# A two-layer decoder step: the first part's last norm woven between the second part's output products, a bias table from 5 products instead of 12, and other ranks for the streams

## The chip, the cores and the metric

The kernel runs on one core of one Trainium2 chip. The metric is device time in microseconds (us), from the first to the last instruction of one execution and the little that lies around it; a lower number is better. Of the kernel before there are three timed runs and one execution recorded by the profiler.

The core has five engines that run side by side, each through its own queue in order: TensorE (PE in the rows, PEld is its weight load), VectorE (DVE), ScalarE (ACT), GpSimd (POOL) and SyncE (SP), which here issues the DMAs. An instruction waits at the head of its queue until semaphores say that its inputs are written and its buffer is free, and everything behind it on that engine waits with it.

## The reference, cut to what matters

Layer 0 mixes tokens by attention, layer 1 by RWKV-7; both attend to 256 memory tokens, gate, and project to the model width of 1024. The work is 512 tokens of a prompt and 8 samples of 4 new tokens, 544 columns in all. What the change touches:

```python
logits = jnp.where(valid[None, None], logits + bias[None, :, None, :], NEG_INF)   # layer 0, attention bias
...
S = S * w_t[:, :, None, :] + sa[..., None] * b_t[:, :, None, :] + v_t[..., None] * k_t[:, :, None, :]  # layer 1
...
h = jnp.concatenate([y, o_mem], axis=-1) * jax.nn.silu(gate)
return h @ w_out, cols[:, -1], S.astype(xn.dtype)
...
xp = xp + rms_norm(hp, norm_post[i])          # after each layer, over the 1024 features
```

The three places are the bias of the samples' new keys in layer 0, the order of layer 1's streams, and layer 1's last norm and residual.

## The kernel before

Activations lie with features on the 128 partitions and the 544 tokens along the free side, so a projection of 1024 to 128 features is eight k-tiles, each of three products: weights and activations are split into a high and a low part (`hi`, `lo`), and `mm1` multiplies high by high, low by high and high by low (L311 to L313). `split_piece` (L297 to L304) loads a weight piece, casts the high part on ACT and subtracts on POOL.

Layer 0 begins with the memory tokens, cross attention and the projections `a{n}`. The bias tables are made on PE at 117 to 124 us, between the products of a projection: `SB` for the cached keys (L715, L716) and `SN` for the samples' new keys. For `SN` the kernel runs over two groups of 4 samples (`bg`) and three window groups (`j`); each pair takes a product of the table `lg` with a one-hot block (L722) and a product of the mask `negsel` with `bad` (L723), each of 32 columns. All of these are plain fp32, so each shows twice in the trace.

Layer 1 is a set of generators, called streams, each with a rank. The planner `Flow` picks the stream with the lowest rank that is ready, advances a clock by the time that the stream states, and so writes one program; `LAT` holds the delays after which a stream counts as ready again, `RANK` the ranks, `GORDER` the order of the eight gate columns, `GEARLY` how many of them may come before the last column. The engines then run the written order. For each of three groups of four heads (`g` = 0, 1, 2) the streams are:

- `scores`, `products`: the chunk matrices `SA`, and their triangular inverse by 30 steps on DVE, two instructions per step (`TX`, L1445, and `T`, L1447);
- `recur`: the state `St` over 8 chunks, with products `z` and `y` (L1631);
- `sample`: the samples' states (`zs`, `us`, `sts`, L1594), then their norm; `norm`, `normed`: the group norm of `y`, written to `bv`.

The dense work that fills PE between them is the columns `b{n}`, the gates `b1{j}_` and, at the end, the output projection. `outer` prepares its inputs: `gated(j)` reads the gate `ug{j}` back from DRAM, multiplies (L1757, DVE), casts to `h1` (L1758, ACT) and subtracts the low part (L1759, on DVE for `j` in `LOD`, else on POOL). The `o1` products use heads of groups 0 and 1; `last(i)` adds those of group 2 for part `i` of the tokens (0: 256 columns, 1: 288): eight products `o2{mt}{i}` added to `z` on DVE (L1791), squares on ACT (L1793), their sum on POOL (L1796) and PE (L326), the reciprocal root (`pow`, L339, on POOL; `rvx`, L346, on ACT; `rs_p`, L353, on PE), and for each of eight tiles a multiplication (L1805, DVE), the residual's addition (L1806, on DVE for `kt` in `RADD`, else on POOL) and an output DMA (L1807, issued by SP).

In `last` the finish of part 0 stands as one block, ahead of the products of part 1 in the program:

```python
rp = rstd_of(acc, n, lambda name: zs[:, 512:1024] if i else ps_t(name), f"p1{i}", eps=4e-6)
yield 0.2, 2.0
for kt in range(8):
    nc.vector.scalar_tensor_tensor(z[kt], z[kt], vec("post1", kt), rp, ALU.mult, ALU.mult)
    (nc.vector if kt in RADD else nc.gpsimd).tensor_tensor(z[kt], z[kt], xr[kt], ALU.add)
    nc.sync.dma_start(O["y"][:, kt, ts], z[kt])
```

Of the kernel before, what the change touches and what calls it, by code (L numbers as in the profile page):

```python
# [16 lines left out]
ALU = mybir.AluOpType  # L17
# [4 lines left out]
TMPB = 6  # L22
WLV = (2, 3, 4, 7)
SQB, XNB = 9, 2
GORDER = (6, 2, 0, 1, 7, 3, 4, 5)
COLB = 5
HB = 3
RAWB = 2
RAWO = 3
XRB = 14  # L30
OFF = {0: 0, 8: 0, 9: -200, 10: -200}
SQ1 = 6
RADD = (0, 3, 6)
ET = mybir.EngineType
D, A, G = ET.DVE, ET.Activation, ET.Pool
MENG = set(), set(), set()
# [1 line left out]
LOP = (0, 3, 4)  # L38
WOB = 10
DU = 2  # L40
GEARLY = 7
LAT = [4.0, 5.82, 0.4, 0.6, 5.42, 5.2, 1.5, 0.94, 2.61, 0.6, 1.2]
RANK = [4, 2, 7, 3, 2, 4, 6, 9]
RHO, DEBT = 0.35, 0.5
LOD = [7]
KB = 4
CCB = 8
PB_ = 4
# [6 lines left out]
PART = (slice(0, 256), slice(256, NT))  # L55
# [3 lines left out]
GORD = (1, 2, 0)  # L59
# [170 lines left out]
def _device(tc, I, O):  # L230
# [20 lines left out]
    def ps_t(name):  # L251
        return psum[0].tile([128, 512], F32, tag="t", bufs=2, name=name)
# [30 lines left out]
    def vec(name, j):  # L283
        s = PV[name]
        return pv[:, s.start + j:s.start + j + 1]
# [36 lines left out]
    def add_squares(acc, sq, n, first, last):  # L322

        for i in (0, 256, 128) if n > 256 else (0, 128):
            w = min(128, n - i)
            nc.tensor.matmul(acc[0:w, i // 128:i // 128 + 1], sq[:, i:i + w], ones[:, 0:1],  # L326
                             start=first and i == 0, stop=last and i == 128)
# [30 lines left out]
    def rstd_of(acc, n, bank, name, out=None, eps=1e-6):  # L358
        return rstd_end(rstd_mid(rstd_begin(acc, n, name, eps), n, name), n, bank(f"rs_{name}"), out)
# [319 lines left out]
    with ExitStack() as pro:  # L679
        pm = pool(pro, "bias", 1)  # L680

        ohp = pm.tile([33, 9 * 256], F32, name="ohp")
        rel = pm.tile([33, 12], F32, name="rel")
        nc.sync.dma_start(ohp, I["ohp"])
        nc.vector.memset(rel[32:33, :], NEG)
        nc.sync.dma_start(rel[0:32, :], I["rel"])
        bv = pm.tile([4, 9 * 256], F32, name="bv")
        for a, b, g in ((0, 512, 0), (512, 1024, 0), (1024, 1536, 0), (1536, 1792, 0), (1792, 2048, 1), (2048, 2304, 2)):
            ps = ps_t(f"bv{a}")
            nc.tensor.matmul(ps[0:4, :b - a], rel[:, g * 4:g * 4 + 4], ohp[:, a:b], start=True, stop=True)  # L690
            nc.vector.tensor_copy(bv[:, a:b], ps[0:4, :b - a])
        bd = pdr.tile([4, 9 * 256], F32, name="bd")
        nc.sync.dma_start(bd, bv)
        for h in range(4):
            t = bd[h:h + 1, :]
            nc.sync.dma_start(PB[:, h].rearrange("p (m k) -> p m k", m=9),
                              bass.AP(tensor=t.tensor, offset=t.offset, ap=[[1, 128], [256, 9], [1, 128]]))

        ohs = pm.tile([128, 1248], F32, name="ohs")
        bad = pm.tile([32, 1248], F32, name="bad")  # L700
        negsel = pm.tile([32, 256], F32, name="negsel")
        rel4 = pm.tile([128, 12], F32, name="rel4")
        dt4 = pm.tile([128, 4], F32, name="dt4")
        lg = pm.tile([128, 3, 4, 8, 4], F32, name="lg")
        for t, n in ((ohs, "ohs"), (bad, "bad"), (negsel, "negsel"), (rel4, "rel4"), (dt4, "dt4")):
            nc.sync.dma_start(t, I[n])
        nc.vector.memset(lg, 0.0)
        for g in range(3):
            nc.vector.tensor_tensor(
                lg[:, g, :, 0:4, :],  # L710
                rel4[:, None, g * 4:g * 4 + 4, None].to_broadcast([128, 4, 4, 4]),
                dt4[:, None, None, :].to_broadcast([128, 4, 4, 4]), ALU.mult)
        for g, a, b in ((1, 0, 512), (2, 512, 1024), (0, 1024, 1152)):
            ps = ps_t(f"sb{g}")
            nc.tensor.matmul(ps[:, :b - a], lg[:, g].rearrange("p a b c -> p (a b c)"), ohs[:, a:b], start=True, stop=False)  # L715
            nc.tensor.matmul(ps[:, :b - a], negsel[:, 0:128], bad[:, a:b], start=False, stop=True)  # L716
            nc.scalar.copy(SB[:, a:b], ps[:, :b - a])
        for bg in range(2):
            ps = ps_t(f"sn{bg}")
            for j, g in enumerate(GORD):  # L720
                a = 1152 + 32 * j
                nc.tensor.matmul(ps[:, 32 * j:32 * j + 32], lg[:, g].rearrange("p a b c -> p (a b c)"), ohs[:, a:a + 32], start=True, stop=False)  # L722
                nc.tensor.matmul(ps[:, 32 * j:32 * j + 32], negsel[:, bg * 128:bg * 128 + 128], bad[:, a:a + 32], start=False, stop=True)  # L723
            nc.scalar.copy(SN[:, bg], ps[:, :96])

    def attention(f, pat):

# [381 lines left out]
    def tmp(name):  # L1109
        return pp.tile([128, NT], F32, tag="tmp", bufs=TMPB, name=name)  # L1110
# [656 lines left out]
            rows.append(tmp(f"{name}7")[:, 0:n])  # L1767
        return t, rows

    def last(i):  # L1770

        n, ts = (256, 288)[i], PART[i]
        z, h1 = out.z[i], out.h1
        t, xr = by_row(i, "SA", 2048, "xr1")
        m = 7 + (not i)
        nc.sync.dma_start(t[:, 0:m * n].rearrange("p (k t) -> p k t", t=n), x1d[:, 0:m, ts])
        if i:
            nc.sync.dma_start(xr[7], x1d[:, 7, ts])
        for j in (4, 5):
            gated(j, (i,))  # L1780
        yield 0.0, 2.0
        zs = ps_zs("ssz11") if i else None
        acc = zs[:, 0:512] if i else ps_t("ssz10")
        sqs = []
        for mt in range(8):
            ps = ps_mm(f"o2{mt}{i}")
            for k in range(2):
                a = (mt % 2 * 2 + k) * 128
                mm1(ps, out.w2h[:, mt // 2, a:a + 128], out.w2l[:, mt // 2, a:a + 128],
                    h1[:, 0, 4 + k, ts], h1[:, 1, 4 + k, ts], n, k == 0, k == 1)  # L1790
            nc.vector.tensor_tensor(z[mt], z[mt], ps[:, :n], ALU.add)  # L1791
            sq = tmp(f"sqo1{mt}{i}")[:, 0:n]
            nc.scalar.activation(sq, z[mt], AF.Square)  # L1793
            sqs.append(sq)
            if 0 < mt < SQ1:
                nc.gpsimd.tensor_tensor(sqs[0], sqs[0], sq, ALU.add)  # L1796
            if mt > SQ1:
                add_squares(acc, sqs[mt - 1], n, mt == SQ1 + 1, False)
            yield 0.75, 0.2
        add_squares(acc, sqs[0], n, False, False)  # L1800
        add_squares(acc, sqs[7], n, False, True)
        rp = rstd_of(acc, n, lambda name: zs[:, 512:1024] if i else ps_t(name), f"p1{i}", eps=4e-6)
        yield 0.2, 2.0
        for kt in range(8):
            nc.vector.scalar_tensor_tensor(z[kt], z[kt], vec("post1", kt), rp, ALU.mult, ALU.mult)  # L1805
            (nc.vector if kt in RADD else nc.gpsimd).tensor_tensor(z[kt], z[kt], xr[kt], ALU.add)  # L1806
            nc.sync.dma_start(O["y"][:, kt, ts], z[kt])  # L1807
            yield 0.0, 0.7

    def outer():  # L1810
# [129 lines left out]
```

## Time and profile before

| what | us |
| --- | --- |
| median of three runs | 816.17 (813.39 to 816.59) |
| the profiled execution's own time | 817.52 |
| its span, first to last instruction | 815.7 |
| PE busy | 757.4 (93%) |
| DVE busy | 465.9 (57%) |
| POOL busy | 351.4 (43%) |
| ACT busy | 338.9 (42%) |

The busy times are sums over the whole span. The profile cuts the span into 40 slices of about 20 us; a digit is the busy share of a slice in tenths, and the row PEclk gives the clock that the throttle granted to TensorE, also in tenths of full speed. Full speed is 2.4 GHz, half is 1.2 GHz. 1.82 us of the execution lie outside the span.

### The profile page before, as it was taken

The numbers are of one execution on the slowest core, as the hardware profiler recorded it, in microseconds if no ns is written. First come the engines' busy times: TensorE is split into PE (matmuls) and PEld (weight loads), VectorE is DVE, ScalarE is ACT, GpSimd is POOL, SyncE is SP. The second block draws the span as 40 slices with busy tenths as digits, with TensorE's granted clock in tenths as the row PEclk, the third lists the DMA queues.
The fourth block names the chain that finished last, engine by engine and source line by source line (L and its number), as shares of the span: only waits on it lengthen the run. The fifth ranks groups of instructions, "written<-read, shape, count | busy, mean of one in ns | idle before, by whom it ended". The sixth has DMA issues, their size and how long they took to land.

```text
span 815.7 us, 20095 instructions
## 1 busy us (share of the span) xinstructions
PE 757.4 (93%) x8278; PEld 643.7 (79%) x8278; DVE 465.9 (57%) x1095; ACT 338.9 (42%) x780; POOL 351.4 (43%) x388
## 2 busy tenths in 40 slices
PE   6999999999998997989999999999989999699883
PEld 5877778889875785678988889888879988498773
DVE  7643311237457556664365478945599547862485
ACT  7445311224344345435876446523545233223031
POOL 4642222332220064754543346635366345543264
PEclk9999998999999999999999999999999999689996
DMA  7473386872221565217213442210223233423013
GB/s 244 135 243 120 113 263 220 297 252 80 79 68 57 228 187 195 65 54 239 61 60 102 148 131 81 73 42 28 69 82 95 81 107 103 147 78 101 2 45 103
DMA packets 59089, 99.51 MB, mean 122 GB/s; under 512 B 6416, under 2 KB 24112, under 8 KB 58960
## 3 DMA queue, kind: packets, MB, share of 16 engines
q1 hardware_dynamic: 58996, 98.22, 36.9%
q8 instruction: 65, 1.06, 0.5%
q14 instruction: 28, 0.22, 0.1%
HBM read 84.15 MB, written 14.05 MB: 120 GB/s over the span
## 4 chain that ended last, share of the span: by engine, by line
PE 69%; DVE 15%; POOL 5%; DMA 4%; ACT 3%; issue 3%; SPq 1%; DVEq 0%; POOLq 0%; ACTq 0%
PE o L311 2%; PE o L313 2%; PE Sx L558 2%; PE b_h L311 2%; PE o L312 2%; PE b_h L312 1%; PE o L772 1%; PE y L1631 1%; PE b_h L313 1%; PE sc L1368 1%; PE z L1631 1%; PE ox L582 1%; PE pa L764 1%; PE ptx L574 1%; PE sA L802 1%
## 5 line engine op out<-in xcount | busy, mean ns | idle before, releaser
L304 POOL TENSOR_TENSOR lo_b<-raw_b,hi_b 128x512 fp32r<-128x512 f32 x58 | 77.0, 1329 | 117.7 <-ACT hi_b L303 80.9
L304 POOL TENSOR_TENSOR lo_a<-raw_a,hi_a 128x512 fp32r<-128x512 f32 x44 | 57.1, 1299 | 146.1 <-ACT hi_a L303 144.9
L303 ACT CAST hi_a<-raw_a 128x512 fp32r<-128x512 f32 x44 | 27.3, 620 | 68.3 <-DMA raw_a<-in_w_in_a 7.0
L303 ACT CAST hi_b<-raw_b 128x512 fp32r<-128x512 f32 x58 | 36.2, 625 | 36.5 <-PE b_h L313 11.0
L311 PE MATMUL b_h<-xg,hi_b 128*128 128x272 f32 x160 | 46.9, 298 | 0.8 <-DVE xv L1136 0.5
L312 PE MATMUL b_h<-xg,lo_b 128*128 128x272 f32 x160 | 46.0, 295 | 0.0
L313 PE MATMUL b_h<-xg,hi_b 128*128 128x272 f32 x160 | 45.4, 291 | 0.0
L1445 DVE TENSOR_TENSOR TX<-T,TT 128x30 f32<-128x30 f32 (+14 forms) x90 | 29.4, 327 | 4.9 <-ACT T L1419 3.0
L311 PEld LDWEIGHTS b_h<-xg,hi_b 128*128 128x128 f32 x160 | 29.8, 188 | 2.7 <-issue 1.2
L1447 DVE TENSOR_TENSOR T<-T,TX 128x30 f32<-128x30 f32 (+14 forms) x90 | 30.1, 334 | 2.3 <-DVE TX L1445 0.4
L312 PEld LDWEIGHTS b_h<-xg,lo_b 128*128 128x128 f32 x160 | 29.8, 189 | 0.3
L313 PEld LDWEIGHTS b_h<-xg,hi_b 128*128 128x128 f32 x160 | 29.7, 188 | 0.2
L1673 POOL TENSOR_TENSOR Sd<-St,DF 128x128 f32<-128x128 f32 x21 | 8.5, 402 | 34.0 <-DVE St L1689 23.1
L311 PE MATMUL o<-h,hi_o1a 128*128 128x256 f32 (+1 forms) x64 | 20.4, 332 | 1.7 <-ACT h L1758 1.7
L749 ACT ACTIVATE P<-P,m 128x768 f32<-128x768 f32 x16 | 14.9, 935 | 16.3 <-DVE m L748 16.3
L313 PE MATMUL o<-h,hi_o1a 128*128 128x256 f32 (+1 forms) x64 | 20.0, 328 | 0.3
L312 PE MATMUL o<-h,lo_o1a 128*128 128x256 f32 (+1 forms) x64 | 19.3, 313 | 0.0
L764 PE MATMUL pa<-ident,P 128*128 128x128 f32 x96 | 14.4, 281 | 3.6 <-DVE P L751 1.4
L1368 PE MATMUL sc<-AR,BK 64*64 64x128 f32 x384 | 17.3, 276 | 0.0
L765 ACT COPY PT<-pa 128x512 f32<-128x512 f32 x16 | 9.3, 582 | 16.5 <-PE pa L764 14.5
L764 PEld LDWEIGHTS pa<-ident,P 128*128 128x128 f32 x96 | 10.6, 142 | 6.7 <-issue 2.3
L1671 DVE TENSOR_TENSOR UV<-z,UV 128x128 f32<-128x128 f32 x21 | 6.0, 287 | 17.1 <-PE z L1631 16.9
(1057 smaller groups left out, 2848.9 us busy)
## 6 DMA issues: line engine op xcount, KB each, us to landing
raw_b<-in_w_in_b SPq DMA_DIRECT2D x58, 256.0 KB, 2.7
raw_a<-in_w_in_a SPq DMA_DIRECT2D x44, 256.0 KB, 2.7
kc<-in_kc SPq DMA_DIRECT2D x18, 512.0 KB, 5.3
vc<-in_vc SPq DMA_DIRECT2D x18, 512.0 KB, 6.1
out_win<-t SPq DMA_DIRECT2D x12, 272.0 KB, 2.8
PB<-bd SPq DMA_DIRECT2D x4, 576.0 KB, 6.8
x<-in_x SPq DMA_DIRECT2D x8, 272.0 KB, 6.3
xr<-in_x SPq DMA_DIRECT2D x16, 136.0 KB, 4.5
```

The costliest lines, as they stand in the source:

```text
L303: nc.scalar.copy(hi, raw)
L304: lo_eng.tensor_tensor(lo, raw, hi.bitcast(F32), ALU.subtract)
L311: nc.tensor.matmul(ps[:, :n], hi, xh, start=first, stop=False)
L312: nc.tensor.matmul(ps[:, :n], lo, xh, start=False, stop=False)
L313: nc.tensor.matmul(ps[:, :n], hi, xl, start=False, stop=last)
L558: nc.tensor.matmul(S[hh][64 * e:64 * e + 64, 0:256], qm[r, f, a:a + 64], kT[l][r, f, :], start=True, stop=True)
L749: nc.scalar.activation(P, P, AF.Exp, bias=m1[:, 0:1], scale=1.0, accum_out=m1[:, 1:2])
L764: nc.tensor.transpose(dst, P[:, j * 128:j * 128 + 128], ident)
L1368: nc.tensor.matmul(pts[e][unit(c, j, h)[0], a:a + 128], BK[H2[h], j, x, CH[c]], AR[H2[h], j, :, CH[c]], start=True, stop=True)
L1445: nc.vector.tensor_tensor(pd, TP[:, 0:s, s:s + 1].to_broadcast([128, s, w]), TT[:, s:s + 1, s + 1:32].to_broadcast([128, s, w]), ALU.mult)
L1447: nc.vector.tensor_tensor(TP[:, 0:s, s + 1:32], TP[:, 0:s, s + 1:32], pd, ALU.add)
L1631: nc.tensor.matmul(out, lhs, rhs, start=start, stop=stop)
```

## The change

Five edits. (1) The `SN` table: one bank holds both sample groups; the mask is added by two products of 96 columns, and the three one-hot products write both groups at once, 2 x 32 columns each. One copy on ACT follows instead of two. (2) `last(0)` stops after its `rvx`; `last(1)` makes `rp0` on PE after its second product, and calls `finish(0, ...)` for one tile after each of the products 3, 5 and 7 (`FIN`), and for the five that are left while the norm of part 1 is on its way. `turn` stamps the order of these DVE instructions. (3) `RADD` is (0,) instead of (0, 3, 6): of each part's eight additions one is on DVE and seven are on POOL. (4) `LOD` is (6, 0, 2) instead of (7,): DVE takes three of the low-part subtractions, POOL the others. (5) `GORDER`, `GEARLY`, three entries of `LAT` and `RANK` differ, so the planner writes another order of the streams.

```diff
-GORDER = (6, 2, 0, 1, 7, 3, 4, 5)
+GORDER = (6, 2, 4, 0, 7, 3, 5, 1)
...
+FIN = 3, 5, 7
 SQ1 = 6
-RADD = (0, 3, 6)
+RADD = (0,)
...
-RANK = [4, 2, 7, 3, 2, 4, 6, 9]
+RANK = [7, 2, 7, 3, 2.5, 2.5, 3, 9]
 RHO, DEBT = 0.35, 0.5
-LOD = [7]
+LOD = (6, 0, 2)
...
+        ps = ps_t("sn")
         for bg in range(2):
-            ps = ps_t(f"sn{bg}")
-            for j, g in enumerate(GORD):
-                a = 1152 + 32 * j
-                nc.tensor.matmul(ps[:, 32 * j:32 * j + 32], lg[:, g].rearrange("p a b c -> p (a b c)"), ohs[:, a:a + 32], start=True, stop=False)
-                nc.tensor.matmul(ps[:, 32 * j:32 * j + 32], negsel[:, bg * 128:bg * 128 + 128], bad[:, a:a + 32], start=False, stop=True)
-            nc.scalar.copy(SN[:, bg], ps[:, :96])
+            nc.tensor.matmul(ps[:, 96 * bg:96 * bg + 96], negsel[:, bg * 128:bg * 128 + 128], bad[:, 1152:1248],
+                             start=bg == 0, stop=False)
+        for j, g in enumerate(GORD):
+            a = 1152 + 32 * j
+            nc.tensor.matmul(ps[:, 0:192].rearrange("p (x c) -> p x c", x=2)[:, :, 32 * j:32 * j + 32],
+                             lg[:, g].rearrange("p a b c -> p (a b c)"), ohs[:, None, a:a + 32].to_broadcast([128, 2, 32]),
+                             start=False, stop=j == 2)
+        nc.scalar.copy(SN, ps[:, 0:192].rearrange("p (x c) -> p x c", x=2))
...
+    def finish(i, rp, kt, xr):
+
+        z, ts = out.z[i], PART[i]
+        nc.vector.scalar_tensor_tensor(z[kt], z[kt], vec("post1", kt), rp, ALU.mult, ALU.mult)
+        turn()
+        if kt in RADD:
+            nc.vector.tensor_tensor(z[kt], z[kt], xr[kt], ALU.add)
+            turn()
+        else:
+            nc.gpsimd.tensor_tensor(z[kt], z[kt], xr[kt], ALU.add)
+        nc.sync.dma_start(O["y"][:, kt, ts], z[kt])
...
+            if i and mt == 1:
+                rp0 = rstd_end(out.rvx, 256, ps_t("rs_p10"))
+            if mt in FIN and left:
+                finish(0, rp0, left.pop(0), out.xr)
             yield 0.75, 0.2
...
+        rv = rstd_begin(acc, n, "p11", 4e-6)
+        turn()
+        rvx = rstd_mid(rv, n, "p11")
+        yield 0.2, 0
+        while left:
+            finish(0, rp0, left.pop(0), out.xr)
+        rp = rstd_end(rvx, n, zs[:, 512:1024])
```

DVE in the tail, before: `z10` and `z11` are the sums of parts 0 and 1, `o2{mt}1` the products of part 1, `rs_p10` the reciprocal root of part 0, `xr10` the residual.

```order
L1791 TENSOR_TENSOR z11_9630<-z11_9630,o211_10200 128x288
L1805 SCALAR_TENSOR_TENSOR z10_9629<-z10_9629,pv_76,rs_p10_10152 128x256 x8
L1806 TENSOR_TENSOR z10_9629<-z10_9629,xr10_10042 128x256
L1791 TENSOR_TENSOR z11_9630<-z11_9630,o221_10211 128x288
L1806 TENSOR_TENSOR z10_9629<-z10_9629,xr10_10042 128x256
L1791 TENSOR_TENSOR z11_9630<-z11_9630,o231_10222 128x288
```

And DVE in the same place after the change.

```order
L1811 TENSOR_TENSOR z11_9621<-z11_9621,o221_10178 128x288
L1811 TENSOR_TENSOR z11_9621<-z11_9621,o231_10189 128x288
L1781 SCALAR_TENSOR_TENSOR z10_9620<-z10_9620,pv_76,rs_p10_10175 128x256
L1784 TENSOR_TENSOR z10_9620<-z10_9620,xr10_10033 128x256
L1811 TENSOR_TENSOR z11_9621<-z11_9621,o241_10203 128x288
L1811 TENSOR_TENSOR z11_9621<-z11_9621,o251_10214 128x288
L1781 SCALAR_TENSOR_TENSOR z10_9620<-z10_9620,pv_76,rs_p10_10175 128x256
L1811 TENSOR_TENSOR z11_9621<-z11_9621,o261_10228 128x288
```

The eight multiplications of part 0 stood together ahead of the third product's addition; now all eight additions of part 1 have at most two instructions of part 0 ahead of them, and five multiplications stand behind part 1's `rv_p`.

POOL at the end of the program, before: `sqo` are the squares, `rv_p11` the `pow` of part 1.

```order
L1796 TENSOR_TENSOR sqo101_10198<-sqo101_10198,sqo111_10208 128x288
L1806 TENSOR_TENSOR z10_9629<-z10_9629,xr10_10042 128x256 x5
L1796 TENSOR_TENSOR sqo101_10198<-sqo101_10198,sqo121_10219 128x288
L1796 TENSOR_TENSOR sqo101_10198<-sqo101_10198,sqo131_10230 128x288
L1796 TENSOR_TENSOR sqo101_10198<-sqo101_10198,sqo141_10241 128x288
L1796 TENSOR_TENSOR sqo101_10198<-sqo101_10198,sqo151_10252 128x288
L339 TENSOR_TENSOR rv_p11_10284<-rv_p11_10284,mhalf_80 128x3
L1806 TENSOR_TENSOR z11_9630<-z11_9630,xr11_10179 128x288 x4
L1806 TENSOR_TENSOR z17_9631<-z17_9631,xr17_10180 128x288
```

POOL at the same place after the change.

```order
L1787 TENSOR_TENSOR z10_9620<-z10_9620,xr10_10033 128x256
L1817 TENSOR_TENSOR sqo101_10162<-sqo101_10162,sqo151_10222 128x288
L1787 TENSOR_TENSOR z10_9620<-z10_9620,xr10_10033 128x256
L340 TENSOR_TENSOR rv_p11_10260<-rv_p11_10260,mhalf_80 128x3
L1787 TENSOR_TENSOR z10_9620<-z10_9620,xr10_10033 128x256 x5
L1787 TENSOR_TENSOR z11_9621<-z11_9621,xr11_10143 128x288 x6
L1787 TENSOR_TENSOR z17_9622<-z17_9622,xr17_10144 128x288
```

Behind the `pow` of part 1 POOL had five additions; now it has twelve, five of part 0 and seven of part 1. The squares of part 1 no longer wait behind additions of part 0, but for two.

DVE in the inverse of group 2 before, at its 15th and 16th step; `ug2` and `ug3` are the gate products of heads that the first `o1` products need.

```order
L1445 TENSOR_TENSOR TX2_8504<-T2_8507,TT2_8503 128x240
L1757 SCALAR_TENSOR_TENSOR ug2_9614<-bv2_6068,pv_76,ug2_9614 128x544
L1437 TENSOR_TENSOR SAs2_7604<-SAs2_7604,n21_8802 32x64 x2
L1447 TENSOR_TENSOR T2_8507<-T2_8507,TX2_8504 128x15x16
L1445 TENSOR_TENSOR TX2_8504<-T2_8507,TT2_8503 128x240
L1757 SCALAR_TENSOR_TENSOR ug3_9619<-bv3_6844,pv_76,ug3_9619 128x544
L1447 TENSOR_TENSOR T2_8507<-T2_8507,TX2_8504 128x16x15
```

And after the change.

```order
L1557 SCALAR_TENSOR_TENSOR bv2_6059<-gn1s_8399,pv_76,bv2_6059 128x32
L1557 SCALAR_TENSOR_TENSOR bv3_6771<-gn1s_8399,pv_76,bv3_6771 128x32
L1449 TENSOR_TENSOR TX2_8495<-T2_8498,TT2_8494 128x234
L1761 SCALAR_TENSOR_TENSOR ug2_9600<-bv2_6059,pv_76,ug2_9600 128x544
L1761 SCALAR_TENSOR_TENSOR ug3_9615<-bv3_6771,pv_76,ug3_9615 128x544
L1451 TENSOR_TENSOR T2_8498<-T2_8498,TX2_8495 128x18x13
L1443 COPY TX2_8495<-n20_8666 32x64
L1763 TENSOR_TENSOR h1_9443<-ug2_9600,h1_9443 128x544
L1449 TENSOR_TENSOR TX2_8495<-T2_8498,TT2_8494 128x228
```

`ug2` and `ug3` moved from the 15th and 16th step to the 18th, and the low part of head pair 2 came to DVE behind them.

## Rows read from the trace of the kernel before

**Rows 1.** The page's parts 1 and 2: busy time by engine, granted clock by slice.

```profile
PE 757.4 (93%) x8278; PEld 643.7 (79%) x8278; DVE 465.9 (57%) x1095; ACT 338.9 (42%) x780; POOL 351.4 (43%) x388
...
PEclk9999998999999999999999999999999999689996
```

**Rows 2.** PE's waits, 128 to 330: total, times, longest (us).

```profile
PE o0w L311 <- ACT sqoz L967: 2.4, 2, 1.9
```

**Rows 3.** PE's timeline from 118 us: start, us, engine, line, operation, out<-in, shapes.

```profile
118.31 0.30 PE L722 MATMUL sn<-ohs,lg 128*128 128x32 f32 x2
...
120.22 0.39 PE L313 MATMUL a6h<-xg,hi_a 128*128 128x272 f32 x1
...
121.20 0.47 PE L722 MATMUL sn<-ohs,lg 128*128 128x32 f32 x2
...
124.42 0.59 PE L311 MATMUL a6h<-xg,hi_a 128*128 128x272 f32 x1
```

**Rows 4.** Windows: us, then PE, PEld, DVE, ACT, POOL busy, PEclk, DMA, GB/s.

```profile
118.30:121.00 2.70, 2.70 (x21) 2.45 (x19) 0.00 (x0) 0.24 (x1) 0.00 (x0) 1.00 1.20 308
121.50:128.00 6.50, 6.50 (x27) 6.12 (x28) 0.08 (x1) 0.86 (x2) 0.40 (x1) 0.50 0.46 180
...
698.50:718.00 19.50, 15.94 (x72) 12.94 (x72) 16.33 (x42) 3.80 (x7) 7.72 (x8) 0.50 0.41 125
...
797.50:800.50 3.00, 3.00 (x15) 3.00 (x14) 1.49 (x3) 1.26 (x3) 2.11 (x4) 0.50 0.52 173
```

**Rows 5.** Timeline of the tail; in brackets the idle time before, and its releaser.

```profile
792.07 3.22 DVE L1805 SCALAR_TENSOR_TENSOR z<-z,pv,rs_p 128x256 f32<-128x256 f32 x8 [0.40 <-PE rs_p L353]
...
796.51 0.40 PE L311 MATMUL o<-h,w2h 128*128 128x288 f32 x1 [2.05 <-DVE z L1791]
...
801.54 0.45 DVE L1791 TENSOR_TENSOR z<-z,o 128x288 f32<-128x288 f32 x1 [0.38 <-PE o L313]
...
804.30 0.86 POOL L339 TENSOR_TENSOR rv_p<-rv_p,mhalf 128x3 f32<-128x3 f32 x1 [3.10 <-DVE rv_p L338]
...
806.79 3.49 DVE L1805 SCALAR_TENSOR_TENSOR z<-z,pv,ssz 128x288 f32<-128x288 f32 x8 [2.57 <-PE ssz L353]
...
810.19 2.30 DVE L1806 TENSOR_TENSOR z<-z,xr 128x288 f32<-128x288 f32 x3
```

**Rows 6.** Groups by line and shape, 786 to 816: busy us, mean ns | idle before.

```profile
L1806 POOL TENSOR_TENSOR z<-z,xr 128x288 f32<-128x288 f32 x5 | 4.0, 833 | 2.6 <-DVE z L1805 2.6
L1806 POOL TENSOR_TENSOR z<-z,xr 128x256 f32<-128x256 f32 x5 | 3.7, 770 | 0.0
L1791 DVE TENSOR_TENSOR z<-z,o 128x288 f32<-128x288 f32 x8 | 3.5, 449 | 4.1 <-PE o L313 4.1
```

**Rows 7.** Groups by line and shape, 684 to 728, around the inverse of group 2.

```profile
L1759 POOL TENSOR_TENSOR h<-ug,h 128x544 fp32r<-128x544 f32 x5 | 6.7, 1337 | 7.1 <-ACT h L1758 7.1
...
L1758 ACT CAST h<-ug 128x544 fp32r<-128x544 f32 x6 | 3.9, 648 | 11.7 <-DVE ug L1757 9.4 <-DMA ug<-ud 2.3
...
L1837 DVE COPY z<-o 128x256 f32<-128x256 f32 x4 | 1.7, 424 | 3.5 <-PE o L313 3.5
```

**Rows 8.** DVE's timeline, the one low part of a gated head pair there.

```profile
698.94 0.71 DVE L1759 TENSOR_TENSOR h<-ug,h 128x544 fp32r<-128x544 f32 x1
```

**Rows 9.** PE's waits, 684 to 728.

```profile
PE o L311 <- ACT h L1758: 2.7, 5, 0.8
```

**Rows 10.** The page's part 5: one of the two instructions of an inverse's step.

```profile
L1445 DVE TENSOR_TENSOR TX<-T,TT 128x30 f32<-128x30 f32 (+14 forms) x90 | 29.4, 327 | 4.9 <-ACT T L1419 3.0
```

**Rows 11.** PE's timeline at the end of the recurrence.

```profile
779.95 1.05 PE L1594 MATMUL sts<-UX,BKs 64*64 64x512 f32 x4
...
786.88 0.33 PE L1545 MATMUL gn2s<-ident,yc2s 64*64 64x64 f32 x4 [0.55 <-DVE yc2s L1533]
```

**Rows 12.** PE's waits, 330 to 684: on the samples' norm of group 0.

```profile
PE b17h L311 <- DVE gst0s L1526: 1.2, 1, 1.2
```

**Rows 13.** The page's part 6: a weight load, KB, us from issue to landing.

```profile
raw_b<-in_w_in_b SPq DMA_DIRECT2D x58, 256.0 KB, 2.7
```

More of the change, by code (lines that the diff above doesn't have):

```diff
@@ L40 @@
 DU = 2
-GEARLY = 7
-LAT = [4.0, 5.82, 0.4, 0.6, 5.42, 5.2, 1.5, 0.94, 2.61, 0.6, 1.2]
-RANK = [4, 2, 7, 3, 2, 4, 6, 9]
+GEARLY = 4
+LAT = [4.0, 5.82, 0.81, 0.51, 5.42, 5.2, 1.5, 0.94, 1.83, 0.6, 1.02]
+RANK = [7, 2, 7, 3, 2.5, 2.5, 3, 9]
 RHO, DEBT = 0.35, 0.5
-LOD = [7]
+LOD = (6, 0, 2)
 KB = 4
@@ L1768, in by_row, with turn, last @@
         return t, rows
-    def last(i):
+    def turn():
+        tc.stamp_issue_order_token(flow.last(ET.DVE), "last")
+    def finish(i, rp, kt, xr):
[8 more added lines that the diff above has]
+        nc.sync.dma_start(O["y"][:, kt, ts], z[kt])
+    def last(i, before=None):
         n, ts = (256, 288)[i], PART[i]
@@ L1783, in last @@
         acc = zs[:, 0:512] if i else ps_t("ssz10")
-        sqs = []
+        sqs, left = [], list(range(8)) if i else []
         for mt in range(8):
@@ L1801, in last @@
         add_squares(acc, sqs[7], n, False, True)
-        rp = rstd_of(acc, n, lambda name: zs[:, 512:1024] if i else ps_t(name), f"p1{i}", eps=4e-6)
+        if not i:
+            out.rvx, out.xr = rstd_mid(rstd_begin(acc, n, "p10", 4e-6), n, "p10"), xr
+            return
+        rv = rstd_begin(acc, n, "p11", 4e-6)
+        turn()
+        rvx = rstd_mid(rv, n, "p11")
[3 more added lines that the diff above has]
+        rp = rstd_end(rvx, n, zs[:, 512:1024])
         yield 0.2, 2.0
         for kt in range(8):
-            nc.vector.scalar_tensor_tensor(z[kt], z[kt], vec("post1", kt), rp, ALU.mult, ALU.mult)
-            (nc.vector if kt in RADD else nc.gpsimd).tensor_tensor(z[kt], z[kt], xr[kt], ALU.add)
-            nc.sync.dma_start(O["y"][:, kt, ts], z[kt])
+            finish(1, rp, kt, xr)
             yield 0.0, 0.7
```

## The prediction

> **What bounds the kernel now.** I read the page's sums and clock row first. PE is busy for 757.4 of 815.7 us, DVE for 465.9, POOL for 351.4 [rows 1]: as a whole, PE bounds. The clock row shows where PE has work but not its speed: it stands at 9 but for an 8 in the slice from 122 us, a 6 and an 8 in the two from 693, and a 6 in the last [rows 1]. Then I read PE's waits by stretch. From 128 to 330 us the costliest single group is 2.4 us in 200 [rows 2]: here a microsecond of PE work removed is a microsecond off the end. Then the timeline of each edited place, and windows over it for the clock.
>
> Three stretches are not PE-bound. Around the inverse of group 2, from 698.5 to 718, the clock is 0.50 of full, which is 1.2 GHz, DVE is busy for 16.33 of 19.5 us, and PE for 15.94 at that half speed [rows 4]: DVE's chain sets the pace, and PE runs dense work beside it. In the tail PE stands still for 2.05 us at 796.51, released by DVE's addition, after DVE had spent 3.22 us on eight multiplications of part 0 [rows 5]. And behind the last addition of part 1 at 801.54 a chain over four engines ends with DVE and POOL at 812.49 (810.19 and 2.30) [rows 5]; about 3.2 us follow it in the span, for the last output.
>
> **The change part by part.** Sums are made against the profiled execution, 817.52 with a span of 815.7. It lies 1.35 above the median of the runs, 816.17, and I carry each difference over to the median.
>
> The bias table. The first half of `SN` takes PE from 118.31 to 120.22, 1.91 us for six products, or 0.32 each; the second from 121.20 to 124.42, 3.22 us or 0.54 each, since PE is at half speed there [rows 3]. The windows show the fall: at 1.00 in 118.3 to 121, at 0.50 in 121.5 to 128 [rows 4]. The dense work from 124.42 to 128.0 thus takes 3.58 us for 1.79 us of work at full speed. Together the table costs 1.91 + 3.22 + 1.79 = 6.92. After: five products, 1.59 at 0.32 each, 2.68 at 0.54; I take 1.8, near the lower, for the two with 96 columns are longer. What the clock does decides the rest. If it doesn't fall, 6.92 - 1.8 = 5.1 is saved. If it falls for a stretch as short as one in the tail, the 3.0 us at 0.50 from 797.5 [rows 4], 1.5 of it is lost again: 3.6. If it falls for 6.5 us as now, 3.25 is lost: 1.9; with slow products on top 1.0. I take -3.6, the case in the middle (ends -5.1 and -1.0). PE is busy in 100% of both windows, so nothing hides or eats it. The copy on ACT that goes away is off the path: ACT is busy 0.24 of 2.70 us there [rows 4].
>
> On the clock the Trainium skill ("TensorE: Matmul & The Clock Gate", What's actually happening) names the throttled state as the default, which activity of the engine releases. By that rule a table of fewer, wider products gives less reason to fall back, and the term would be nearer -5.1 than -3.6; the trace agrees in the place of the fall, behind the first six products of 32 columns, and can't show what five wider ones do.
>
> The weave. DVE's eight multiplications no longer stand ahead of part 1's additions, so PE's 2.05 us of idle time goes. The products behind it ran at 0.50, PE busy for all 3.00 us of the window [rows 4]; fed without a break they may keep the full clock, which would save up to 1.5; I take 1.0 of it. So the eighth product's addition comes 3.05 us earlier, at 798.5 for 801.54, and POOL's `pow`, now at 804.30 for 0.86 [rows 5], runs from 801.25 to 802.1. By the queue's order POOL then has five additions of part 0, 0.74 each (3.7 for five), and seven of part 1, 0.80 each (4.0 for five) [rows 6]: 3.7 + 5.6 = 9.3. Its last ends at 811.4 in place of 812.49, -1.1. Ends: -1.6 with all of the 1.5, +0.2 if only 1.75 us is gained. The three multiplications and the addition that are woven in lie beside PE's products: DVE is busy for 1.49 of the 3.00 us there [rows 4]; without that cover they cost some 0.4 each. SP still issues sixteen outputs; the five of part 0 that now come late are ahead of part 1's in its queue, and POOL's 0.74 each spaces them. DVE's last eight multiplications start earlier than 806.79 and hide behind POOL. POOL, not DVE, is late next, by the count of its additions.
>
> The gated inputs around the inverse. DVE takes over two more low parts: 2 x 0.71 [rows 8] = 1.42; one copy `z` less, 0.42 [rows 7]. POOL needs 1.337 for the same, and the five there waited 7.1 us for ACT's casts [rows 7]: POOL loses work that costs nothing. On SP the reloads of the gates 7 and 0 come earlier and two states' loads later, which nothing here prices but the stall below. Heads 2 and 3 are multiplied some three steps of the inverse later (from the 15th and 16th to the 18th); a step is two instructions of 0.33 [rows 10] with the gaps around them. PE has waited 2.7 us for those casts [rows 9], and DVE 3.5 us for the `o1` products that it copies [rows 7]. If DVE's work lies wholly on its chain and nothing is given back, that is +1.0, and 2.0 us for the later heads, +3.0 in all; with 2.7 more for the `o1` products' wait, +5.7; with the copies' 3.5 gone, 1.0 - 3.5 = -2.5. I take +1.5, nearest to DVE's own row.
>
> The end of the recurrence. Two blocks of sample products, 1.05 at 779.95 [rows 11], go into earlier PE work, and the samples' norm goes ahead of the last head's, which frees part of the wait of 0.55 at 786.88 [rows 11]. The end shortens by 1.05 and up to twice that; moved work costs the same where PE is full. I take -1.5 (ends 0 and -2.1), since PE is not full in the tail. From 330 to 684 the planner's order changes at the group norm; the wait of 1.2 there [rows 12] may go or stay: -0.6 (ends 0 and -1.2).
>
> Sum: -3.6 - 1.1 + 1.5 - 1.5 - 0.6 = -5.3. That is 812.2 for an execution like the profiled one and 810.9 by the median.
>
> **The rivals.** *The clock doesn't fall at all, and the loop runs without a delay.* For it: the stretch before is at 1.00 with PE busy throughout, and only the 32-column products precede the fall. Against it: five such products remain. -5.1 - 1.1 + 0 - 2.1 - 0.6 = -8.9, 807.3.
>
> *The clock falls as long as now.* For it: five narrow products remain, in the same place. Against it: they take a third of the time. The bias term is then -1.9 for -3.6: 812.6. The step is right and the size wrong.
>
> *The weave gives nothing and POOL becomes the end.* DVE's woven instructions stand in its queue ahead of the additions that free PE's banks, so PE waits as before and the `pow` still ends at 805.16 (804.30 and 0.86 [rows 5]); the 9.3 behind it end at 814.5 for 812.49, +2.0 in place of -1.1: -2.2 in all, 814.0. For it: five additions of part 0, which ran beside other work before 797, now lie behind the `pow`. Against it: never more than two instructions of part 0 stand together, 0.8 us where it was 3.22 [rows 5]. The Trainium skill ("GPSIMD Engine Reference", 4.1 Engine selection) advises VectorE for an elementwise addition, POOL being about twice as slow with two inputs; the trace bears that out with 0.833 against DVE's 0.449 [rows 6], and by that rule this rival is the likely one.
>
> *The loop stalls: slower.* In the written order DVE may now wait for a reload of `ug` and for ACT's cast at each low part: two loads of the size of a weight's, 2.7 us each [rows 13], and three times a cast of 0.648 [rows 7] with the subtraction of 0.71 behind it, 4.1, make 9.5 us. PE's `o1` products stand in order behind those heads, and a clock held at half for 6.5 us more costs 0.82 x 6.5 / 2 = 2.7 (0.82 is its busy share there [rows 4]). 12.2 in place of +1.5 gives +5.4, 821.6. It decides from 6.8 us, where the sum passes nothing. For it: ACT's casts already wait 9.4 us for DVE's `ug` [rows 7]. Against it: DVE waits little for loads, and the order has other work between each pair.
>
> **How the numbers follow.** Chances: forecast 0.48, with its own range 808 to 814; clock never falls 0.16; clock as long as now 0.15; POOL the end 0.11; the stall 0.10. A measurement of this kernel tells about 0.5%, or 4.1 us, from no change: faster means below 812.1, slower above 820.3. Of the forecast about 0.38 lies below 812.1, of the first rival 0.15, of the second 0.05, of the third 0.02: 0.60. Slower holds nearly all of the stall, 0.09; 0.31 is left. The range runs from 804, for the first rival with its bounds, to 818, short of the stall.
>
> **What would show it.** The bias: five products ahead of a granted clock of 1.00 (rival one), half for about 3 us (forecast) or 6.5. The weave: no idle time of PE above 0.5 us between the products of part 1, the `pow` 2 to 3.6 us earlier against the last product, twelve POOL additions back to back behind it. The loop: the cast of head 3 on ACT no more than 3 us later against the start of the inverse; a wait of DVE for `ug` or `h` of over 1 us there is the stall. The end: the four 64x512 products no longer between the last `y` and the samples' norm. The forecast is wrong if the inverse's stretch is longer by over 6 us, or if the time before 330 us isn't 2 us or more shorter.

## The result, and the profile after

The changed kernel takes 809.21 us in the median of nine runs (807.35 to 812.99), beside 814.94 for before (nine runs, 812.38 to 816.59). The ratio is 0.9941, with an interval of 0.9921 to 0.9961: 4.8 us less, 3.2 to 6.4. The forecast was 5.3 less, 810.9. The sum came out; its terms did not.

The page of the kernel after, busy time and clock by slice, answers to [rows 1]:

```profile
PE 751.7 (93%) x8264; PEld 637.4 (79%) x8264; DVE 463.0 (57%) x1093; ACT 338.6 (42%) x779; POOL 353.3 (44%) x390
...
PEclk9999999999999999999999999999999999689997
```

PE is 5.7 us less busy, and the 8 in the slice from 122 us is a 9. The table's place in PE's timeline (start, us, engine, line, operation) answers to [rows 3]:

```profile
118.92 0.68 PE L721 MATMUL sn<-bad,negsel 32*128 32x96 f32 x4
119.53 0.88 PE L725 MATMUL sn<-ohs,lg 128*128 128x64 f32 x6
120.22 0.37 PE L314 MATMUL a6h<-xg,hi_a 128*128 128x272 f32 x1
```

The windows (PEclk is the third number from the end) answer to [rows 4]:

```profile
118.30:121.00 2.70, 2.70 (x20) 2.46 (x21) 0.00 (x0) 0.58 (x2) 0.00 (x0) 1.00 1.08 306
121.50:128.00 6.50, 6.50 (x53) 4.91 (x53) 1.92 (x4) 1.24 (x2) 2.74 (x3) 1.00 0.65 242
```

Five products take 1.30 us, 0.26 each, and the clock stays at its upper level behind them: 53 matmuls in a window that held 27. The tail, answering to [rows 5]:

```profile
790.40 0.40 PE L312 MATMUL o<-h,w2h 128*128 128x288 f32 x1 [0.20 <-DVE z L1811]
...
792.30 0.46 DVE L1811 TENSOR_TENSOR z<-z,o 128x288 f32<-128x288 f32 x1 [0.35 <-PE o L314]
...
795.18 0.86 POOL L340 TENSOR_TENSOR rv_p<-rv_p,mhalf 128x3 f32<-128x3 f32 x1 [1.23 <-DVE rv_p L339]
796.01 8.90 POOL L1787 TENSOR_TENSOR z<-z,xr 128x256 f32<-128x256 f32 x12
...
799.01 3.05 DVE L1781 SCALAR_TENSOR_TENSOR z<-z,pv,ssz 128x288 f32<-128x288 f32 x7
```

PE's wait of 2.05 us is 0.20, DVE ends at 802.06, and POOL's twelve additions run without a gap to 804.91, where DVE's additions had ended at 812.49. The rest of layer 1 is read from four instructions: the end of the last product of column 1 (`b1h`, a dense column of layer 1; the expectations below call it the second gate column), the start and end of the inverse of group 2, and the first product of part 1. In the trace of before (the inverse's start and end were not among the rows ahead):

```profile
440.28 0.29 PE L313 MATMUL b1h<-xg,hi_b 128*128 128x272 f32 x1
686.50 0.19 DVE L1445 TENSOR_TENSOR TX<-T,TT 128x30 f32<-128x30 f32 x1 [1.99 <-ACT T L1419]
723.44 0.20 DVE L1447 TENSOR_TENSOR T<-T,TX 128x30 f32<-128x30 f32 x1
788.60 0.54 PE L311 MATMUL o<-h,w2h 128*128 128x288 f32 x2
```

And after:

```profile
431.41 0.29 PE L314 MATMUL b1h<-xg,hi_b 128*128 128x272 f32 x1
684.29 0.19 DVE L1449 TENSOR_TENSOR TX<-T,TT 128x30 f32<-128x30 f32 x1 [0.79 <-ACT T L1423]
717.84 0.20 DVE L1451 TENSOR_TENSOR T<-T,TX 128x30 f32<-128x30 f32 x1
783.19 0.83 PE L312 MATMUL o<-h,w2h 128*128 128x288 f32 x2
```

The inverse starts 252.6 us after that product in place of 245.9, lasts 33.75 in place of 37.14, part 1 begins 65.15 behind it in place of 64.96, and from there it is 24.3 to the end of the span in place of 27.1. So after is 6.7 us later at the start of the inverse than the column before it would have it, and gets 3.4 of that back in the inverse: a loss that no term of the forecast had. 1.2 of the 6.7 is a fall of the clock in after's trace at 516 us (0.57 from 516 to 520), where the order is still that of before.

The two spans, 815.7 and 807.5, lie 8.2 apart, more than the times do. 2.35 of it is one place near 350 us where the trace of before is late against that of every other kernel here; such scatter is why terms are compared below between fixed instructions, over all traces.

### The profile page after: what moved, and what is told of

Read it like the earlier page. It is cut to its first block, busy times and chain, and to the rows that moved or that the text cites. A ratio compares the mean times of both kernels' runs of the same rounds, so it can differ in the third digit from the quotient of the medians.

```text
span 807.5 us, 20072 instructions
## 1 busy us (share of the span) xinstructions
PE 751.7 (93%) x8264; PEld 637.4 (79%) x8264; DVE 463.0 (57%) x1093; ACT 338.6 (42%) x779; POOL 353.3 (44%) x390
## 4 chain that ended last, share of the span: by engine, by line
PE 74%; DVE 13%; DMA 4%; ACT 3%; POOL 3%; issue 1%; SPq 0%; POOLq 0%; ACTq 0%; DVEq 0%
PE o L312 3%; PE o L313 2%; PE b_h L312 2%; PE o L314 2%; PE b_h L313 2%; PE b_h L314 2%; PE sc L1372 2%; PE y L1635 2%; PE z L1635 2%; PE Sx L559 2%; PE o L776 1%; PE ox L583 1%; PE pa L768 1%; PE ptx L575 1%; POOL z L1787 1%
## 5 line engine op out<-in xcount | busy, mean ns | idle before, releaser
L312 PE MATMUL o<-h,hi_o1a 128*128 128x256 f32 (+1 forms) x64 | 19.2, 313 | 1.6 <-ACT h L1762 1.6
L1372 PE MATMUL sc<-AR,BK 64*64 64x128 f32 x384 | 19.2, 281 | 0.2 <-DVE bv L1318 0.2
L314 PE MATMUL o<-h,hi_o1a 128*128 128x256 f32 (+1 forms) x64 | 18.7, 309 | 0.0
L1281 POOL TENSOR_TENSOR rv<-rv,mhalf 128x10 f32<-128x10 f32 x6 | 14.0, 2336 | 3.9 <-DVE rv L1280 3.9
L1372 PEld LDWEIGHTS sc<-AR,BK 64*64 64x64 f32 x384 | 13.4, 136 | 2.9 <-issue 0.8
```

Source lines behind the costliest of these rows:

```text
L312: nc.tensor.matmul(ps[:, :n], hi, xh, start=first, stop=False)
L314: nc.tensor.matmul(ps[:, :n], hi, xl, start=False, stop=last)
L1372: nc.tensor.matmul(pts[e][unit(c, j, h)[0], a:a + 128], BK[H2[h], j, x, CH[c]], AR[H2[h], j, :, CH[c]], start=True, stop=True)
```

## The experiments

The first four kernels each had one part of the change.

**The table alone, order left free.** The hunk on `SN` of the diff, in the kernel before.

> Kernel before with the bias table alone made from five products. Theory (the clock no longer falls behind the table, as in the profile after): all of the 12 products' time beyond five and of the half-speed stretch is gone, PE is 5.5 us earlier from 126 us on, and, since PE is full from there to 330 us, the kernel is 5 us faster: 809.9 where before is 814.9. Rival 1 (the forecast's size, a short fall): 3.6 us. Rival 2 (the table is off the end's path, later waits eat it): PE is 5.5 us earlier at 200 us but under 2 us earlier at 684 us, and the time is within 2 us of before.

814.37 us, ratio 1.0006 (0.9981 to 1.0032). PE was 5.47 us earlier behind the table and had lost none of it at 510 us; then it did. The theories argue over one program with one table or the other, and it was another program: from some 550 us on the order of instructions differs, in some 880 of 6021 rows of PE. The program's last stage sorts each engine's queue by a simulated clock (`schedule_with_timeline_sim=True`, L1921), and seven products fewer move that clock. The inverse starts 251.6 us behind column 1, and part 1 begins 67.9 us behind the inverse.

**The weave alone.** The hunks on `last`, `finish`, `FIN`, `RADD`. PE's order differs from before in 4 rows.

> Kernel before with the weave and with one addition on DVE in place of three; table and streams' ranks as before. Theory: PE's 2.05 us of idle time and the half-speed stretch among part 1's products are gone, the pow comes 3.7 us earlier against the start of part 1, twelve additions on POOL follow it and give 1.5 back: 2.2 us faster, 812.7. Rival (POOL as the end takes it all): the pow is earlier, the last addition isn't, within 0.5 us of before.

813.41 us, ratio 0.9998 (0.9973 to 1.0024): 2.2 us faster is the end of the interval, no change its middle. In the trace the tail did as the theory said, and this execution lost time at the old table, at half clock for longer than before's 6.5 us:

```profile
121.00:131.00 10.00, 10.00 (x42) 9.55 (x42) 0.19 (x1) 1.10 (x3) 1.27 (x1) 0.50 0.34 131
```

**The weave with three additions on DVE.**

```diff
-RADD = (0,)
+RADD = (0, 3, 6)
```

> As the run with the weave, but with three additions of each part on DVE, as before. Theory: the additions of part 0 on DVE stand ahead of part 1's products' additions, two at a time at most; POOL has four additions fewer behind the pow (the tiles 3 and 6 of each part, two of them late), so the last addition ends about 1.5 us earlier than in the run with the weave: 3.7 us faster than before, 811.2. Rival: DVE's additions beside POOL take 0.8 as on POOL and delay DVE's eight multiplications, so that nothing is won against the run with the weave, 812.7.

814.25 us, ratio 1.0000 (0.9978 to 1.0022), and no gain in the tail: 26.74 us from the first product of part 1 to the end, where the weave alone has 24.12. Most of the difference lies ahead of the `pow`, which comes 13.7 us behind that product for 11.8; among the products of part 1 the clock was 0.69 in this execution and 1.00 in that of the weave alone. From the `pow` to the end it is 13.0 us for 12.4, and only this 0.7 is laid to the additions. For it the expectation had counted additions and forgotten the order: `turn` puts each of DVE's additions behind the multiplication of its tile, and they take turns with POOL's. The last of it, DVE and POOL:

```profile
786.10:797.00 10.90, 10.39 (x50) 9.29 (x50) 4.45 (x12) 3.62 (x9) 6.17 (x9) 0.69 0.04 14
...
804.68 1.54 POOL L1784 TENSOR_TENSOR z<-z,xr 128x288 f32<-128x288 f32 x2 [0.82 <-DVE z L1778]
805.49 1.05 DVE L1781 TENSOR_TENSOR z<-z,xr 128x288 f32<-128x288 f32 x1
806.46 1.35 DVE L1778 SCALAR_TENSOR_TENSOR z<-z,pv,ssz 128x288 f32<-128x288 f32 x3
807.04 1.54 POOL L1784 TENSOR_TENSOR z<-z,xr 128x288 f32<-128x288 f32 x2 [0.82 <-DVE z L1778]
```

Each of these additions of DVE takes 1.05 us beside POOL's, and POOL then stands 0.82 for the next multiplication. By the times the run doesn't differ from the weave alone; that the weave pays only with `RADD` is not shown.

**The tables of numbers alone.** `GORDER`, `GEARLY`, `LAT`, `RANK`, `LOD` of the diff, in the kernel before.

> Kernel before with the new ranks, due times, gate order and low-part engines alone; table and tail as before. Theory from the two profiles (after lost some 5 us between 510 and 686 us and won 2.9 in the inverse of group 2 and 1.6 at the recurrence's end): the order moves waits from one stretch to the other and is worth within 1 us of nothing, 815. Forecast's terms: -0.6 from 330 to 684, +1.5 in the inverse, -1.5 at the end: 814.3, with the inverse's stretch longer. Rival (the order is worth as much as the rest): 3 us faster, 812.

827.70 us, ratio 1.0170 (1.0136 to 1.0204): 14 us slower, outside all that was expected. It too has an order of its own, which is neither that of before nor that of after (some 910 rows of PE differ from after); what in it costs the 14 us was not looked into. These two edits thus tell nothing of their terms, as long as each rewrites the rest.

So the order was held. The final order of each engine was read from one build and laid on another as edges between neighbours, which order and don't wait. In the run that follows, every engine's instructions but those of the table stand in the order of before, without exception.

```diff
     with tile.TileContext(nc, schedule_with_timeline_sim=True) as tc:
         _device(tc, ia, oa)
+        _pin(tc)
```

**The table, in the order of before.**

> Kernel before with the five products, and with the order of every engine's other instructions held as in before, instruction by instruction (edges that order and don't wait). Theory (the table's 5.5 us are lost in the free run because the order from 550 us on changed with it): PE stays about 5.5 us ahead to the end, 5 us faster, ratio 0.994. Rival (what the table saves is eaten by later waits, whatever the order): PE is 5.5 us ahead at 500 us, and the time is within 1.5 us of before.

809.15 us, ratio 0.9931 (0.9908 to 0.9955): 5.6 us. The theory held. The same four instructions:

```profile
433.01 0.29 PE L313 MATMUL b1h<-xg,hi_b 128*128 128x272 f32 x1
...
679.29 0.19 DVE L1448 TENSOR_TENSOR TX<-T,TT 128x30 f32<-128x30 f32 x1 [1.99 <-ACT T L1422]
715.94 0.20 DVE L1450 TENSOR_TENSOR T<-T,TX 128x30 f32<-128x30 f32 x1
...
781.63 0.53 PE L311 MATMUL o<-h,w2h 128*128 128x288 f32 x2
```

245.99, 36.85 and 65.49 us, near those of before (245.9, 37.1, 65.0): what the table gives stays.

**The order of after with the old table.**

> Kernel after with the old table of twelve products in two banks, the order of every other instruction held as in after. Theory (table 5.5 us, weave 2, order within 2 of nothing): within 2 us of before, ratio 0.998 to 1.002. Rival (the new order is worth as much as the table, and the two add up only by halves): 3 us or more faster than before, ratio 0.996 or less.

815.50 us, ratio 1.0022 (0.9998 to 1.0045). All of the change but the table is worth nothing, or costs a little.

**The table and the weave, in the order of before.**

> The run with the weave (order of before up to the tail, one addition on DVE) and the five products, order held. Theory: 5.5 of the table and 2.0 of the tail add up, 7 us faster than before, ratio 0.991, and so faster than after, whose new order then costs 1.5. Rival (the new order is needed to keep what the table saves): 3 us faster or less, ratio 0.996 or more.

808.69 us, ratio 0.9942 (0.9916 to 0.9969), between the two: the interval just shuts out the theory's 0.991 and holds the rival's 0.996. Its span, 806.9, is 1.4 under that of the table alone. The theory had it 1.5 us faster than after; the ratios, 0.9942 and 0.9941, show no difference.

**Two more additions on DVE, in after.**

```diff
-        if kt in RADD:
+        if kt in RADD or i and kt in (4, 7):
```

> Kernel after with two more additions of part 1, tiles 4 and 7, on DVE in place of POOL. In the profile after DVE ends at 802.06 and POOL's last addition at 804.91, twelve back to back from 796.01. Theory (POOL's count of additions sets the end): POOL ends two additions, 1.5 us, earlier, DVE as much later, both near 803.5: 1.3 us less from the pow to the end. Rival (both engines slow each other, 0.8 us an addition on either): the last addition as late as in after, within 0.4 us.

808.13 us, ratio 0.9923 (0.9897 to 0.9950). By the trace the theory: POOL's last additions, and DVE's last,

```profile
792.84 0.86 POOL L340 TENSOR_TENSOR rv_p<-rv_p,mhalf 128x3 f32<-128x3 f32 x1 [1.46 <-DVE rv_p L339]
793.67 7.90 POOL L1787 TENSOR_TENSOR z<-z,xr 128x256 f32<-128x256 f32 x10
...
800.46 0.46 DVE L1784 TENSOR_TENSOR z<-z,xr 128x288 f32<-128x288 f32 x1
```

end at 801.57 and 800.92; from the pow to the end of the span it is 11.4 us, where after has 12.3: 0.9 us less, not 1.3.

**All three in the order of before.**

> Order of before up to the tail, held, with the five products, the weave, and the tiles 4 and 7 of part 1 added on DVE besides. Theory (three terms that add up, and the new order left out): table 5.5, tail 2.7, additions 0.7, so 9 us faster than before, ratio 0.989, span near 806; 348 to 350 us from the end of the second gate column's products to the first product of part 1, 23.5 from there to the end. Rival (the terms don't add: what the front gains the tail waits for): ratio 0.993 or more, as with the table alone.

807.31 us, ratio 0.9929 (0.9906 to 0.9952). The front and the tail came as expected (349.5 and 23.5 us), the time did not: 0.989 is outside the interval. Its median is the lowest of all, yet its interval holds the ratios of the table alone and of after.

**After with one low part on DVE.**

```diff
-LOD = (6, 0, 2)
+LOD = [7]
```

> Kernel after with the low part of head pair 7 alone on DVE, as before, in place of 6, 0 and 2. The rest of the order differs from after in 58 of 6021 PE rows. Theory (the low parts on DVE are what the inverse pays): PE's wait for the casts, 5.2 us in after, falls back to 2.7, and the stretch from the second gate column to part 1, 351.5 us in after, is shorter by 1.4 us or more. Rival (the order of the streams costs it, not DVE's two subtractions): the stretch stays at 351 to 352.

812.07 us, ratio 0.9977 (0.9957 to 0.9998): about 2.9 us slower than after, and the theory is turned round. PE's waits from 684 to 728 us:

```profile
PE o L312 <- ACT h L1762: 4.4, 3, 2.9
PE gn1s L1549 <- DVE yc1s L1537: 2.9, 1, 2.9
PE o L314 <- POOL h L1763: 1.2, 1, 1.2
```

With the low parts on POOL a wait of 1.2 us for POOL's `h` appears, the inverse is 34.7 us long for 33.75, and part 1 begins 66.7 behind it for 65.15: 2.6 us in these two. The stretch ahead of the inverse is 3.6 longer too, but it grows before the orders part, and the clock fell there at 524.5 and at 569 us, where after's did not; that part is not put down to the edit.

**Eight products.** Two mask products of 96 columns, six one-hot products of 32, in one bank; order of before.

```diff
+            nc.tensor.matmul(ps[:, 96 * bg:96 * bg + 96], negsel[:, bg * 128:bg * 128 + 128], bad[:, 1152:1248], start=bg == 0, stop=False)
+            for j, g in enumerate(GORD):
+                nc.tensor.matmul(ps[:, 96 * bg + 32 * j:96 * bg + 32 * j + 32], lg[:, g].rearrange("p a b c -> p (a b c)"), ohs[:, a:a + 32], start=False, stop=bg == 1 and j == 2)
```

> Kernel before with eight products in one bank (two mask products of 96 columns, six one-hot products of 32), order of all others held. Each product is about 0.32 us, so the table takes 2.6 us in place of 5.1. Theory (what makes the clock fall is the length of the stretch of narrow fp32 products): with half the stretch the clock stays, and PE is 4.7 us ahead at 131 us; 4.5 us faster, ratio 0.9945. Rival (the number of products of 32 columns decides, six as in the first half of the old table): the clock falls for 6.5 us or more as in before, and PE is 1.3 us ahead.

811.05 us, ratio 0.9982 (0.9957 to 1.0006). Neither came out: the clock fell, but for 3.5 us, and PE was 2.97 us ahead at 131 us.

```profile
120.00:123.50 3.50, 3.50 (x18) 3.50 (x18) 0.19 (x1) 0.32 (x1) 0.00 (x0) 0.52 0.74 290
123.50:127.00 3.50, 3.50 (x30) 3.21 (x33) 0.88 (x2) 0.77 (x2) 1.29 (x1) 1.00 0.02 8
```

Against five products that is 2.5 us lost, of which three products are about 0.9 (an estimate from 0.32 each) and the half-speed stretch the rest.

## Why the prediction was right in its sum and wrong in its terms

All traces side by side, each number between the four instructions shown above, in us:

| kernel | column 1 to inverse | inverse | inverse to part 1 | part 1 to end |
| --- | --- | --- | --- | --- |
| before | 245.9 | 37.1 | 65.0 | 27.1 |
| table, order of before | 246.0 | 36.9 | 65.5 | 26.7 |
| eight products, order of before | 247.2 | 35.7 | 65.9 | 25.4 |
| weave | 247.2 | 35.9 | 65.6 | 24.1 |
| weave, three additions on DVE | 247.1 | 37.0 | 64.9 | 26.7 |
| table and weave, order of before | 246.3 | 36.6 | 66.8 | 24.1 |
| all three, order of before | 246.3 | 36.5 | 66.7 | 23.5 |
| after | 252.6 | 33.8 | 65.2 | 24.3 |
| after, old table | 252.5 | 33.8 | 64.9 | 24.3 |
| after, two more additions on DVE | 251.9 | 34.0 | 65.3 | 23.8 |
| after, one low part on DVE | 256.2 | 34.7 | 66.7 | 24.7 |
| table alone, order free | 251.6 | 34.3 | 67.9 | 26.8 |
| numbers alone | 257.5 | 35.4 | 65.2 | 30.3 |

*The bias table, -3.6 forecast, -5.5 measured.* The step that failed is the choice of the middle case for the clock. There it doesn't fall in any of the seven traces with the five products, and it falls in all five with the twelve, for some 7 us in two and some 10 in three. Between the products ahead of the table and those behind it PE gains 5.47 us against the two (before is one) and 7.0 against the three. The time gains 5.6 with the order held. Two more pairs differ in the table alone, the weave with the old and the new one (0.9998, 0.9942) and the order of after with either (1.0022, 0.9941): 4.6 and 6.6 us, some 3 to either side. That PE is full there and nothing eats it was right. The first rival's mechanism, half of it, is what happened. The Trainium skill ("TensorE: Matmul & The Clock Gate", What's actually happening), by which activity releases the throttled state, would have put the term near -5.1; the trace agrees, with 1.00 behind the five. What it doesn't explain is the fall in before, where PE was busy for all of the 2.70 us ahead of it [rows 4]; why the clock falls there stays open.

*The weave, -1.1 forecast.* The mechanism is as written: the wait gone, no half-speed stretch from 790 to 796, the pow 12.0 us behind part 1's first product where it was 15.7, and POOL late next. Two sizes were off: the pow gained 3.7, not 3.05, and the twelve additions took 8.9, not 9.3. From part 1's first product the end is 2.6 to 3.0 us nearer. Part of that is the clock: among part 1's products it was 0.74 in before and 1.00 in the weave alone, and it was 1.00, too, in the trace with eight products, which has no weave, waits 2.4 us as before did, and has 25.4 us to the end:

```profile
788.60:801.60 13.00, 10.49 (x51) 9.44 (x50) 8.41 (x20) 3.70 (x9) 9.86 (x13) 0.74 0.25 83
783.00:794.00 11.00, 7.74 (x51) 6.72 (x50) 7.74 (x20) 3.72 (x9) 9.53 (x12) 1.00 0.29 98
787.00:796.00 9.00, 8.06 (x51) 6.76 (x50) 4.47 (x12) 3.68 (x9) 6.14 (x8) 1.00 0.06 17
```

(before, eight products, weave alone.) With the clock up in both, the weave is worth 25.4 less 24.1, 1.3 us, by one pair; that it also keeps the clock up, as the forecast took for 1.0 us, is not shown. Some is given back ahead, where part 1 begins later: in the order of before it is 92.1, 92.2 and 91.4 from the inverse's end to the end of the span without the weave (before, and the two tables), 89.8 and 90.9 with it (alone, and with the table), 1.6 us less in the mean. The times, for it alone and on top of the table, show no gain, with 2 to 3 us to either side. The -1.6 is thus the traces' alone.

*The new order, -0.6 in three terms, +2.2 by the traces.* Here the prediction failed: two of the three terms came out with the sign turned round. From column 1 to part 1 the seven traces with the order of before have 348.0 to 349.7 us, the three with that of after 351.2 to 351.5. By stretch, mean against mean: +5.8 ahead of the inverse (forecast -0.6), -2.7 in it (forecast +1.5), and then, with the weave in both, 0.9 us less from its end to the end of the span (forecast -1.5, with 0 and -2.1 as ends). Of the 5.8, 5.5 lies behind the end of column 10 (152.1 to 152.4 us from there to the inverse in the seven, 157.4 to 158.0 in the three); the rest is ahead of where the orders part, and the clock's.

I had looked for waits in the stretch ahead and found few; it has few after, too: from column 10 to the inverse PE is idle for 3.8 us in before, 5.0 in after. What moved is the order: the changed program does 572 dense products there in place of 557, and beside the inverse, where DVE's chain sets the pace, 88 are left in place of 117. Fifteen dense products are some 1.9 us (an estimate from 0.126 between their starts), so that with the idle time about 3 of the 5.5 are accounted for; the rest stays open. PE's waits beside the inverse, answering to [rows 9]:

```profile
PE o L312 <- ACT h L1762: 5.2, 3, 3.6
```

This is 5.2 us where it was 2.7. That the order ahead is traded for idle time in the inverse is read from the rows, not tried by itself.

That the inverse is shorter all the same is DVE's doing. Its copies of the `o1` products, and its multiplications of `ug`, hardly wait any more (before, then after; the last number is the idle time ahead of them):

```profile
L1757 DVE SCALAR_TENSOR_TENSOR ug<-bv,pv,ug 128x544 f32<-128x544 f32 x4 | 3.8, 951 | 1.5 <-DMA ug<-ud 0.9 <-issue 0.6
L1837 DVE COPY z<-o 128x256 f32<-128x256 f32 x3 | 1.3, 425 | 2.2 <-PE o L313 2.2
...
L1761 DVE SCALAR_TENSOR_TENSOR ug<-bv,pv,ug 128x544 f32<-128x544 f32 x4 | 3.6, 916 | 0.2 <-DMA ug<-ud 0.2
L1763 DVE TENSOR_TENSOR h<-ug,h 128x544 fp32r<-128x544 f32 x3 | 2.6, 864 | 0.0
L1869 DVE COPY z<-o 128x256 f32<-128x256 f32 x2 | 0.8, 420 | 0.1
```

3.4 us of waits go, and DVE's two further low parts take 1.9. The prediction had this case, with the copies' wait gone and -2.5, as one end of its term, and chose +1.5 instead.

The times don't show the +2.2. Three pairs differ in the order (and the low parts) alone: table and weave, 0.9942 in the order of before and 0.9941 in after; the weave with the old table, 0.9998 and 1.0022; two more additions, 0.9929 and 0.9923. That is -0.1, +2.0 and -0.5 us for the new order, some 3 to either side each.

*DVE's low parts, +1.0 within the loop's term.* Wrong in sign, by one run. On DVE they make the inverse no longer, and taking them back to POOL costs 2.9 us by the times, with an interval of some 2.5 to either side, and 2.6 in the two stretches named above. I had priced DVE's 1.42 us and called POOL's work free, since POOL waited; but PE waits for its result. The Trainium skill ("GPSIMD Engine Reference", 4.1 Engine selection) prefers VectorE for elementwise work with two inputs; here it agrees, by 0.71 us against 1.34 [rows 7, 8].

The three terms by the traces, -5.5, -1.6 and +2.2, make -4.9; the ratio of the times says -4.8. That the sum came out is luck: against the forecast's terms these are -1.9, -0.5 and +2.8 off, and the errors cancel. The rival *POOL becomes the end* was half true, since POOL ends last; its premise, that the pow stays where it was, was false. The stall of DVE didn't come: no wait of DVE for `ug` over 0.2 us from 680 to 726, and the last cast of the heads began 23.5 us behind the inverse's start, as before.

## What to carry to other kernels

Ask first whether an edit that is small and early changes the order of everything behind it: where the last stage sorts by a simulated clock, single edits can't be told from their new orders until the order is held, and then a part worth 5.6 us shows what it is worth. A time that matches a sum does not confirm its terms, which need an instruction at either end of each. And note the granted clock beside each stretch that is compared: in the tail here it made about as much as the weave did. On an engine that is full, work put earlier is not work saved; by the rows here it was taken from beside the chain that it had covered.

## What was not expected

The fall of TensorE's clock at the old table makes the larger part of what the new one saves, and varies: twelve products at 0.32 us are 3.8, five took 1.3, so that of the 5.5 us some 3 are the clock's (an estimate), and the half-speed stretch lasted some 7 us in two executions and some 10 in three others of the same products. And an addition of 128x288 on DVE, beside POOL's additions, took 0.46 us in one place of the tail and 1.05 in another.
